# The mLSTM state stores of a hybrid diffusion trunk step: both directions of a head in one PSUM tile, one copy and one store each of C and n

## The chip, the cores and the metric

The kernel runs on one core of a Trainium2 chip. The metric is the device time of one execution, in microseconds (us). Profiles come from one profiled execution. In them PE is TensorE's matmul, PEld its weight load, DVE VectorE, ACT ScalarE, POOL GpSimd and SP SyncE, the engine whose queue issues nearly all DMAs of this kernel.

## The reference

One denoising step of one trunk layer, for two groups of tokens: 512 latent tokens of one request (which use a cache of context) and 128 context tokens of another (which start from empty states and leave new ones). The hidden size is 1024, all in fp32. A normalised and modulated input `h` goes through one wide projection `h @ w_in`, whose columns feed four mixers side by side and the gates:

- MLA, attention over a compressed key-value latent;
- mLSTM in both directions, 4 heads with keys of 64 and values of 128;
- windowed attention with grouped heads (SWA);
- RWKV-7 in both directions.

Their outputs are projected, gated and added, and a squared-ReLU MLP follows. The part around the change is the end of the mLSTM, for the context tokens. Per direction and head, with an empty state before, it is

```python
wk    = jnp.exp(g - m_new[..., None])
C_new = decay[..., None, None] * C + jnp.einsum('bhs,bhsd,bhsv->bhdv', wk, kc, vc)
n_new = decay[..., None] * n + jnp.einsum('bhs,bhsd->bhd', wk, kc)
```

so the new C is a product of weighted keys and values (64x128), and the new n the sum of the weighted keys (64). The outputs `new_mlstm_C` and `new_mlstm_n` have the shapes (1, 1, 2, 4, 64, 128) and (1, 1, 2, 4, 64): direction, head, key, value.

## The kernel before, in words

**Products.** Projections in fp32 are made as three products of halves: an operand is split into a high and a low part (`wh` and `wl` of a weight, `HH` and `HL` of `h`), and high by high, low by high and high by low are added in PSUM.

**Weights.** `load_split` (L583 to L594) loads a weight tile of 128x512 into `wr` (three buffers), ACT casts it to `wh` (L589), and DVE or POOL subtracts to get `wl` (L592).

**Stages.** The RWKV section comes first, then the mLSTM (L1208 to L1364), in whose time the windowed attention runs too (L1388 to L1510), then MLA (from L1512), then the gates and output projections, then the MLP. While the mixers run, TensorE has filling work: the gate columns of `h @ w_in`. These are tiles `pb` of 128x320 in PSUM, each 24 matmuls, two halves to a job (pb_4434 and pb_4435 are one job). A job's halves are copied out as `spb` by ACT (L833) and by DVE (L835), and stored to a scratch in DRAM by SP (L837, `gtd` and `mog`). There are two `pb` tiles of PSUM, so that a half can start only when the copy of the same half of the job before it is done.

**The mLSTM heads.** A loop over four heads (h), in a pool of SBUF `mh`. For each head the value tile `vt` (`mvt`) has two more columns of ones, so that one product of weighted keys `kw` (128x64) with `vt[:, 4, :]` (128x130) gives C in columns 0 to 127 and n in column 128. `pkt`, `pyb` and `pcf` share one PSUM tile, "my" of 128x512. At the end of a head, for each direction d: DVE weights the keys (`kw`, L1358), TensorE makes the product `pcf`, ACT copies it to `co` (L1362), and SP stores C (L1363, 64 rows of 512 bytes) and n (L1364, 64 elements of 4 bytes, one from each partition). `co` has one buffer, so the copy of the next direction waits until both stores of the last one have landed. `kw` and `jk` (a scratch that takes the squares of `hd`, whose sum is all that is used) have two buffers.

**After the heads.** When the pools `mp` and `mh` are closed, their SBUF goes to pools of the MLA section. Its first loads `ua` (L1553) go to such memory, so they wait until the last store of `co` has landed. From `ua` DVE copies the rotary columns `akr` (L1554), ACT makes sums of squares (`aj`, L1557 and L1558), DVE scales `ua` (L1561, L1562), and TensorE transposes it (`pal`).

**Order.** The instructions are not run in the order of the code. `order()` (L168 to L483) is a list scheduler: it takes all recorded instructions with their dependencies, gives each a duration from formulas (`cost()`, L127; DMAs by a start, an end and a rate, L38), and at each step places on a free engine the ready instruction with the longest path behind it. A DMA that stores from SBUF has 178.188 us added to that path, and a copy out of PSUM has 100. Every engine then executes its list strictly in that order, SP's list of DMA issues as well; a waiting instruction holds up all that stand behind it on its engine. The scheduler knows a DMA by its bytes alone, so it reckons with one and the same short time for the C stores and the n stores as for other small transfers.

Of the kernel before, what the change touches and what calls it, by code (L numbers as in the profile page):

```python
# [11 lines left out]
F32 = mybir.dt.float32  # L12
# [511 lines left out]
def build(nc, tc, I, O):  # L524
    V, A, G, PE, SY = nc.vector, nc.scalar, nc.gpsimd, nc.tensor, nc.sync
# [11 lines left out]
    def nm(s):  # L537
        uid[0] += 1
        return f"{s}_{uid[0]}"

    def mm(out, lhsT, rhs, start=True, stop=True):
        PE.matmul(out, lhsT, rhs, start=start, stop=stop)  # L542
# [308 lines left out]
    mps = mps_cm.__enter__()  # L851
# [360 lines left out]
    with pools(name="mp", bufs=1) as mp, pools(name="mps2", bufs=1, space=PSUM) as mps:  # L1212
# [54 lines left out]
        with pools(name="mh", bufs=1) as mh_:  # L1267
            for h in range(4):
                ht, rw = h // 2, slice((h % 2) * 64, (h % 2) * 64 + 64)
                if h % 2 == 0:  # L1270
                    qT = mh_.tile([128, T], F32, tag="mq", name=nm("mqT"))
                    kT = mh_.tile([128, T], F32, tag="mk", name=nm("mkT"))
                    SY.dma_start(qT, mqk[ht])
                    SY.dma_start(kT, mqk[2 + ht])
                    qsp = [mh_.tile([128, T], F32R, tag=f"mq{i}", name=nm("msp")) for i in range(2)]
                    ksp = [mh_.tile([128, 2, T], F32R, tag=f"mk{i}", name=nm("msp")) for i in range(2)]
                    split(*qsp, qT)
                    for i in range(2):
                        for x in ksp:
                            G.memset(x[hh[1 - i], i, :].bitcast(F32), 0.0)  # L1280
                        split(*(x[hh[i], i, :] for x in ksp), kT[hh[i]])
                vt = mh_.tile([128, NT, 130], F32, tag="mvt", bufs=2, name=nm("mvt"))
                G.memset(vt[:, :, 128:130], 1.0)
                SY.dma_start(vt[:, :, 0:128], mvd[:, ts_(h)].rearrange("(t p) n -> p t n", p=128))
                c0 = mh_.tile([128, 2, 130], F32, tag="mc0", bufs=2, name=nm("mc0"))
                G.memset(c0, 0.0)
                for d in range(2):
                    SY.dma_start(c0[rw, d, 0:128], I["state_mlstm_C"][0, 0, d, h])
                    SY.dma_start(c0[rw, d, 128:129], I["state_mlstm_n"][0, 0, d, h].unsqueeze(1))
                Mb, qs = [], []  # L1290
                for d in range(2):
                    M_ = mh_.tile([128, T], F32, tag="Mb", bufs=2, name=nm("Mb"))
                    SY.dma_start(M_, mdr[h, d].partition_broadcast(128))
                    e0 = mh_.tile([128, NS], F32, tag="e0", bufs=1, name=nm("e0"))
                    A.activation(e0, M_[:, 0:NS], AF.Exp, scale=-1.0, bias=m0b[:, d * 4 + h : d * 4 + h + 1])
                    q_ = mh_.tile([128, NS], F32, tag="qs", bufs=2, name=nm("qs"))
                    G.tensor_tensor(q_, e0, qT[:, 0:NS], op=ALU.mult)
                    Mb.append(M_)
                    qs.append(q_)
                Ps = []  # L1300
                for i in range(5):
                    nf = 512 - 128 * i if i < 4 else 128
                    nb = 128 * (i + 1) if i < 4 else 128
                    t0 = 0 if i < 4 else NS
                    ps = mps.tile([128, 512], F32, tag="ms", name=nm("pms"))
                    n = 512 if i < 4 else 128
                    mm3(ps[:, :n], [x[:, h % 2, ts_(i)] for x in ksp], [x[:, t0 : t0 + n] for x in qsp])
                    P_ = mh_.tile([128, 640], F32, tag="P", bufs=6, name=nm("P"))
                    o = 128 * i if i < 4 else 0
                    A.activation(P_[:, 0:nf], Mb[0][:, t0 + o : t0 + o + nf], AF.Exp, scale=-1.0, bias=tk[:, i * 16 + h : i * 16 + h + 1])  # L1310
                    A.activation(P_[:, nf : nf + nb], Mb[1][:, t0 : t0 + nb], AF.Exp, scale=-1.0, bias=tk[:, i * 16 + 4 + h : i * 16 + 5 + h])
                    G.affine_select(P_[:, 0:128], P_[:, 0:128], pattern=[[1, 128]], compare_op=ALU.is_ge, fill=0.0, base=0, channel_multiplier=-1)
                    G.affine_select(P_[:, nf + nb - 128 : nf + nb], P_[:, nf + nb - 128 : nf + nb], pattern=[[-1, 128]],
                                    compare_op=ALU.is_ge, fill=0.0, base=0, channel_multiplier=1)
                    V.tensor_tensor(P_[:, 0:nf], P_[:, 0:nf], ps[:, o : o + nf], op=ALU.mult)
                    V.tensor_tensor(P_[:, nf : nf + nb], P_[:, nf : nf + nb], ps[:, 0:nb], op=ALU.mult)
                    Ps.append((P_, nf))
                yo = mh_.tile([128, T], F32, tag="myo", bufs=1, name=nm("yo"))
                for j in range(5):
                    ps = mps.tile([128, 512], F32, tag="mo", name=nm("pmo"))  # L1320
                    for d in range(2):
                        out = ps[:, d * 130 : d * 130 + 130]
                        seq = []
                        if j < 4:
                            seq.append((qs[d][:, ts_(j)], c0[:, d, :]))
                            for i in (range(0, j + 1) if d == 0 else range(j, 4)):
                                P_, nf = Ps[i]
                                o = (j - i) * 128 if d == 0 else nf + j * 128
                                seq.append((P_[:, o : o + 128], vt[:, i, :]))
                        else:  # L1330
                            P_, nf = Ps[4]
                            seq.append((P_[:, d * 128 : d * 128 + 128], vt[:, 4, :]))
                        for n, (l, r) in enumerate(seq):
                            mm(out, l, r, start=(n == 0), stop=(n == len(seq) - 1))
                    dn = mh_.tile([128, 2], F32, tag="dn", bufs=4, name=nm("dn"))
                    A.activation(dn, ps[:, 128:260:130], AF.Abs)
                    V.tensor_tensor(dn, dn, tk[:, j * 16 + 8 + h : j * 16 + 16 : 4], op=ALU.max)
                    V.reciprocal(dn, dn)
                    hd = mh_.tile([128, 128], F32, tag="hd", bufs=2, name=nm("hd"))
                    A.activation(hd, ps[:, 0:128], AF.Copy, scale=dn[:, 0:1])  # L1340
                    V.scalar_tensor_tensor(hd, ps[:, 130:258], dn[:, 1:2], hd, op0=ALU.mult, op1=ALU.add)
                    jk = mh_.tile([128, 128], F32, tag="jk", bufs=2, name=nm("jk"))
                    s_ = mh_.tile([128, 1], F32, tag="s_", bufs=2, name=nm("s_"))
                    A.activation(jk, hd, AF.Square, accum_out=s_)
                    rsqrt(mh_, s_, s_, 128, eps6)
                    V.tensor_scalar(hd, hd, s_, None, op0=ALU.mult)
                    ps = mps.tile([128, 512], F32, tag="my", name=nm("pyb"))
                    transp(ps[:, 0:128], hd)
                    A.activation(yo[:, ts_(j)], ps[:, 0:128], AF.Copy, scale=pk("mln"))
                SY.dma_start(yT[1, h], yo)  # L1350
                ps = mps.tile([128, 512], F32, tag="my", name=nm("pkt"))
                if h % 2 == 0:
                    ktok = mh_.tile([128, 128], F32, tag="ktok", bufs=1, name=nm("ktok"))
                    transp(ps[:, 0:128], kT[:, NS:T])
                    A.copy(ktok, ps[:, 0:128])
                for d in range(2):
                    kw = mh_.tile([128, 64], F32, tag="kw", bufs=2, name=nm("kw"))
                    V.tensor_scalar(kw, ktok[:, rw], tk[:, 80 + d * 4 + h : 81 + d * 4 + h], None, op0=ALU.mult)  # L1358
                    ps = mps.tile([128, 512], F32, tag="my", name=nm("pcf"))
                    mm(ps[0:64, 0:130], kw, vt[:, 4, :])  # L1360
                    co = mh_.tile([64, 130], F32, tag="co", bufs=1, name=nm("co"))
                    A.copy(co, ps[0:64, 0:130])  # L1362
                    SY.dma_start(O["new_mlstm_C"][0, 0, d, h], co[:, 0:128])  # L1363
                    SY.dma_start(O["new_mlstm_n"][0, 0, d, h].unsqueeze(1), co[:, 128:129])  # L1364

    def swap_ap(ap, q, which):
        return ap.rearrange("p h (a b q) -> p h a b q", b=2, q=q)[:, :, :, which, :]
# [516 lines left out]
```

## Time and profile before

| | us |
|---|---|
| runs of the kernel before: median of 3 | 1817.38 |
| lowest, highest of them | 1809.24, 1836.86 |
| the profiled execution: its own time | 1829.33 |
| span in its profile, first to last instruction | 1827.4 |
| TensorE matmul busy in it | 1742.4 (95%) |
| ACT busy | 716.9 (39%) |
| DVE busy | 968.7 (53%) |

The mean granted TensorE clock was 0.96 of full speed. The profiled execution is 12 us longer than the median of the runs. The stores in question lie between 811 and 936 us of the span. The profile's columns: a group or tile row gives the line, engine, operation, output<-input and the count; a timeline row gives the start, the length in us, the engine, the line and in brackets the idle time of that engine ahead of it and what ended it; a chain row the start, the length and what ran; a window row its bounds, then its length, then for PE, PEld, DVE, ACT and POOL the busy time and (x) the number of instructions, then the granted TensorE clock, the busy share of the DMA engines and the GB/s.

### The profile page before, as it was taken

What the parts mean: (1) busy time and instruction counts of PE and PEld (TensorE: products, weight loads), DVE (VectorE), ACT (ScalarE), POOL (GpSimd) and SP (SyncE); (2) the same over time, 40 slices, a digit from 0 to 9 for tenths busy, and PEclk for the clock granted to TensorE, in tenths of its full rate; (3) what the DMA queues carried; (4) which work ended last, traced back from release to release, by engine and by line L of the source; (5) the groups of instructions that cost most, each with busy time, mean ns of one, the idle gap of its engine ahead of it and who ended that gap; (6) DMA issues with size and microseconds to landing.
All of it is one profiled execution on the core that took longest, in us unless ns stands there. A gap on an engine that the chain in (4) does not pass through costs nothing.

```text
span 1827.4 us, 32001 instructions
## 1 busy us (share of the span) xinstructions
PE 1742.4 (95%) x11923; PEld 1551.1 (85%) x11923; DVE 968.7 (53%) x2250; ACT 716.9 (39%) x1711; POOL 471.9 (26%) x488
## 2 busy tenths in 40 slices
PE   6999899999999987999989999899999999999998
PEld 3998788888888876878887999799889899898997
DVE  4236937586363348665548654367744334343342
ACT  5543242333223224675635643354434223132231
POOL 3455543354233223331222211005100010202012
PEclk9999999898679998999999999999999999999999
DMA  8554352344224354533363211576512222222222
GB/s 291 153 180 122 103 132 74 90 118 108 64 59 122 114 170 149 168 89 65 86 159 105 74 41 56 167 253 221 173 45 81 68 77 70 81 76 75 76 74 94
DMA packets 243211, 206.66 MB, mean 113 GB/s; under 512 B 46086, under 2 KB 194360, under 8 KB 243056
## 3 DMA queue, kind: packets, MB, share of 16 engines
q1 hardware_dynamic: 242416, 204.07, 38.2%
q8 instruction: 94, 1.54, 0.4%
q0 software_dynamic: 640, 0.56, 0.1%
q14 instruction: 61, 0.50, 0.1%
HBM read 163.08 MB, written 41.49 MB: 112 GB/s over the span
## 4 chain that ended last, share of the span: by engine, by line
PE 57%; DVE 5%; DMA 5%; ACT 1%; issue 1%; SPq 0%; POOL 0%; POOLq 0%; DVEq 0%; ACTq 0%
PE pb L542 29%; PE pa L542 12%; PE pwo L542 2%; DMA out_new_mlstm_n<-co 2%; PE pst L542 2%; PE pas L542 2%; PE pat L542 2%; PE pat L565 1%; PE pso L542 1%; PE pmo L542 1%; PE psc L542 1%; PE pada L542 1%; DMA wr<-in_w_in 1%; PE pms L542 1%; PE pspt L565 0%
## 5 line engine op out<-in xcount | busy, mean ns | idle before, releaser
L542 PE MATMUL pb<-HH,wh 128*128 128x320 f32 x1328 | 364.1, 325 | 21.8 <-ACT spb L833 10.8
L542 PE MATMUL pb<-HL,wh 128*128 128x320 f32 x1328 | 359.5, 323 | 0.8 <-DVE HL L753 0.8
L542 PE MATMUL pb<-HH,wl 128*128 128x320 f32 x1328 | 356.0, 321 | 0.0
L589 ACT CAST wh<-wr 128x512 fp32r<-128x512 f32 (+2 forms) x298 | 183.5, 618 | 379.9 <-PE pa L542 144.2
L592 POOL TENSOR_TENSOR wl<-wr,wh 128x512 fp32r<-128x512 f32 (+2 forms) x139 | 187.4, 1352 | 415.0 <-ACT wh L589 307.8
L542 PEld LDWEIGHTS pb<-HH,wh 128*128 128x128 f32 x1328 | 237.5, 192 | 33.6 <-ACT spb L833 12.9
L542 PEld LDWEIGHTS pb<-HL,wh 128*128 128x128 f32 x1328 | 236.8, 192 | 7.3 <-issue 4.0
L542 PEld LDWEIGHTS pb<-HH,wl 128*128 128x128 f32 x1328 | 236.4, 192 | 6.3 <-issue 3.5
L592 DVE TENSOR_TENSOR wl<-wr,wh 128x512 fp32r<-128x512 f32 x159 | 117.4, 744 | 200.1 <-ACT wh L589 116.5
L1846 POOL TENSOR_TENSOR x<-x,yt 128x512 f32<-128x512 f32 x40 | 53.6, 1341 | 480.7 <-DVE yt L1845 473.7
L542 PE MATMUL pt<-wh,HH 128*128 128x256 f32 (+2 forms) x360 | 101.7, 318 | 7.8 <-DVE mift L860 5.4
L542 PE MATMUL pa<-wh,fh 128*128 128x512 f32 x320 | 108.1, 393 | 0.0
L542 PE MATMUL pa<-wh,fl 128*128 128x512 f32 x320 | 106.7, 393 | 0.0
L542 PE MATMUL pa<-wl,fh 128*128 128x512 f32 x320 | 104.9, 393 | 0.0
L542 PE MATMUL pt<-wh,HL 128*128 128x256 f32 (+2 forms) x360 | 97.9, 312 | 0.0
L542 PE MATMUL pt<-wl,HH 128*128 128x256 f32 (+2 forms) x360 | 96.8, 310 | 0.0
L1109 POOL TENSOR_SCALAR S<-S,DL 128x128 f32<-128x128 f32 x80 | 56.8, 714 | 126.9 <-DVE S L1124 100.3
L542 PEld LDWEIGHTS pt<-wh,HH 128*128 128x128 f32 x360 | 68.1, 206 | 13.6 <-DVE mift L860 3.0
L835 DVE COPY spb<-pb 128x320 f32<-128x320 f32 x46 | 22.4, 487 | 105.9 <-PE pb L542 105.7
L542 PE MATMUL pst<-VU,Am 128*64 128x64 f32 (+1 forms) x640 | 74.2, 242 | 0.9 <-DVE VU L1118 0.5
L542 PE MATMUL pb<-yh,wh 128*128 128x320 f32 x256 | 64.8, 318 | 10.0 <-ACT yh L1752 6.5
L542 PEld LDWEIGHTS pa<-wh,fh 128*128 128x128 f32 x320 | 60.1, 188 | 13.4
(535 smaller groups left out, 3587.0 us busy)
## 6 DMA issues: line engine op xcount, KB each, us to landing
wr<-in_mlp_w SPq DMA_DIRECT2D x128, 256.0 KB
wr<-in_w_in SPq DMA_DIRECT2D x122, 256.0 KB
wa<-in_ada_w SPq DMA_DIRECT2D x64, 256.0 KB
gtd<-spb SPq DMA_DIRECT2D x32, 320.0 KB
sg<-gtd SPq DMA_DIRECT2D x32, 320.0 KB
ara<-in_ada_w SPq DMA_DIRECT2D x16, 512.0 KB
sgd<-sg SPq DMA_DIRECT2D x16, 320.0 KB
la<-sgd SPq DMA_DIRECT2D x16, 320.0 KB
```

Of the source, the lines that this page charges most:

```text
L542: PE.matmul(out, lhsT, rhs, start=start, stop=stop)
L565: PE.transpose(out, in_, ident[: in_.shape[0], : in_.shape[0]])
L589: A.copy(hi[:, :n], raw[:, :n])
L592: e.tensor_tensor(lo[:, :n], raw[:, :n], hi[:, :n].bitcast(F32), op=ALU.subtract)
L835: V.tensor_copy(t[:, hs(h)], p)
L1109: G.tensor_scalar(sn, so_, DL[:, c : c + 1], None, op0=ALU.mult)
L1846: G.tensor_tensor(x2[tt][:, cs], x2[tt][:, cs], t, op=ALU.add)
```

## The change

The products of the two directions go to one PSUM tile, side by side in columns 0 to 129 and 130 to 259. One ACT copy takes both to a tile `co` of 64x2x130, which has two buffers. One DMA stores both directions' C (64x2x128), and one both directions' n (64x2x1). `kw` and `jk` have one buffer instead of two. The numbers over the four heads:

| | before | after |
|---|---|---|
| `kw` on DVE, `pcf` products (128x64 by 128x130) | 8, 8 | 8, 8 |
| `co` copies on ACT | 8 of 64x130 | 4 of 64x260 |
| C stores | 8 of 64x128 | 4 of 64x2x128 |
| n stores | 8 of 64 elements | 4 of 128 elements |

```diff
-                    jk = mh_.tile([128, 128], F32, tag="jk", bufs=2, name=nm("jk"))
+                    jk = mh_.tile([128, 128], F32, tag="jk", bufs=1, name=nm("jk"))
...
+                ps = mps.tile([128, 512], F32, tag="my", name=nm("pcf"))
                 for d in range(2):
-                    kw = mh_.tile([128, 64], F32, tag="kw", bufs=2, name=nm("kw"))
+                    kw = mh_.tile([128, 64], F32, tag="kw", bufs=1, name=nm("kw"))
                     V.tensor_scalar(kw, ktok[:, rw], tk[:, 80 + d * 4 + h : 81 + d * 4 + h], None, op0=ALU.mult)
-                    ps = mps.tile([128, 512], F32, tag="my", name=nm("pcf"))
-                    mm(ps[0:64, 0:130], kw, vt[:, 4, :])
-                    co = mh_.tile([64, 130], F32, tag="co", bufs=1, name=nm("co"))
-                    A.copy(co, ps[0:64, 0:130])
-                    SY.dma_start(O["new_mlstm_C"][0, 0, d, h], co[:, 0:128])
-                    SY.dma_start(O["new_mlstm_n"][0, 0, d, h].unsqueeze(1), co[:, 128:129])
+                    mm(ps[0:64, d * 130 : d * 130 + 130], kw, vt[:, 4, :])
+                co = mh_.tile([64, 2, 130], F32, tag="co", bufs=2, name=nm("co"))
+                A.copy(co, ps[0:64, 0:260].rearrange("p (d n) -> p d n", n=130))
+                SY.dma_start(O["new_mlstm_C"][0, 0, :, h].rearrange("d k v -> k d v"), co[:, :, 0:128])
+                SY.dma_start(O["new_mlstm_n"][0, 0, :, h].rearrange("d k -> k d").unsqueeze(2), co[:, :, 128:129])
```

Since the scheduler starts from other instructions, the order of all engines differs from the first head's stores to the gate stage; before and behind that it is the same. Two places follow.

**The last head's stores and the load of `ua`.** On SP before (a number behind a name is that of the tile; a `gtd` or `mog` store carries the `spb` tile that it stores):

```order
L588 DMA wr_4600<-in_w_in 128x4x128
L1363 DMA out_new_mlstm_C<-co_9699 64x128
L1364 DMA out_new_mlstm_n<-co_9699 64x1
L837 DMA gtd<-spb_4301 128x640
L588 DMA wr_4636<-in_w_in 128x4x128
L1363 DMA out_new_mlstm_C<-co_9707 64x128
L1364 DMA out_new_mlstm_n<-co_9707 64x1
L588 DMA wr_4666<-in_w_in 128x4x128
L1553 DMA ua_10870<-mld 128x416
L1553 DMA ua_10899<-mld 128x416
```

On SP now:

```order
L588 DMA wr_4570<-in_w_in 128x4x128
L1350 DMA yT<-yo_9527 128x640
L1363 DMA out_new_mlstm_C<-co_9687 64x2x128
L1364 DMA out_new_mlstm_n<-co_9687 64x2x1
L588 DMA wr_4600<-in_w_in 128x4x128
L837 DMA gtd<-spb_4301 128x640
L588 DMA wr_4636<-in_w_in 128x4x128
L1553 DMA ua_10850<-mld 128x416
L1553 DMA ua_10879<-mld 128x416
```

One pair of stores stands there instead of two, the load of `wr_4600` has moved behind it, and that of `wr_4666` has moved behind the `ua` loads. On ACT before, at the same place (`spb_4367` is the copy of pb_4368, `spb_4433` that of pb_4434):

```order
L833 COPY spb_4301<-pb_4302 128x320
L1362 COPY co_9699<-pcf_9697 64x130
L589 CAST wh_4533<-wr_4534 128x512
L1362 COPY co_9707<-pcf_9705 64x130
L589 CAST wh_4569<-wr_4570 128x512
L833 COPY spb_4367<-pb_4368 128x320
L589 CAST wh_4599<-wr_4600 128x512
L1557 ACTIVATE aj_10873,asa_10874<-ua_10870 128x256
L1558 ACTIVATE aj_10873,asa_10874<-ua_10870 128x128
L833 COPY spb_4433<-pb_4434 128x320
```

On ACT now, from the copy of pb_4368 on; the one copy `co_9687` stands four rows ahead of it:

```order
L833 COPY spb_4367<-pb_4368 128x320
L1557 ACTIVATE aj_10853,asa_10854<-ua_10850 128x256
L1558 ACTIVATE aj_10853,asa_10854<-ua_10850 128x128
L1557 ACTIVATE aj_10882,asa_10883<-ua_10879 128x256
L1558 ACTIVATE aj_10882,asa_10883<-ua_10879 128x128
L1596 ACTIVATE kj_11855,krr_11854<-akr 128x32
L572 ACTIVATE rst_10859<-rsv_10858 128x2
L1596 ACTIVATE kj_11960,krr_11959<-akr 128x32
L573 ACTIVATE asa_10854<-rst_10859 128x2
L589 CAST wh_4599<-wr_4600 128x512
L572 ACTIVATE rst_10888<-rsv_10887 128x2
```

The cast of `wr_4600` moved from ahead of the first `ua` work to behind it, and the copy of pb_4434 from between the first `ua` tile's work and the second's to behind both (four rows behind the last one shown).

**The first uses of `ua` on DVE and PE.** On DVE before (`spb_4367` here is the copy of pb_4369, the second half of the job):

```order
L835 COPY spb_4301<-pb_4303 128x320
L835 COPY spb_4367<-pb_4369 128x320
L1554 COPY akr<-ua_10870 128x32
L1554 COPY akr<-ua_10899 128x32
L1559 TENSOR_SCALAR asa_10874<-asa_10874 128x1
```

On DVE now:

```order
L1359 TENSOR_SCALAR kw_9684<-ktok_9437,mtk 128x64
L835 COPY spb_4301<-pb_4303 128x320
L1554 COPY akr<-ua_10850 128x32
L1554 COPY akr<-ua_10879 128x32
L835 COPY spb_4367<-pb_4369 128x320
```

The two copies out of `ua` stand ahead of the copy of pb_4369 instead of behind it. On PE before, around the first transposes of `ua`:

```order
L542 MATMUL pb_4501<-HL,wh_4503 128x320
L542 MATMUL pb_4500<-HL,wh_4533 128x320
L565 MATMUL pal_10869<-k_68,ua_10870 128x128 x3
L542 MATMUL pb_4501<-HH,wl_4502 128x320
L542 MATMUL pb_4500<-HH,wl_4532 128x320
L542 MATMUL pb_4501<-HH,wh_4503 128x320
```

On PE now:

```order
L542 MATMUL pb_4435<-HH,wh_4437 128x320
L542 MATMUL pb_4434<-HH,wl_4466 128x320
L565 MATMUL pal_10849<-k_68,ua_10850 128x128 x3
L542 MATMUL pb_4435<-HL,wh_4437 128x320
L542 MATMUL pb_4434<-HH,wh_4467 128x320
L542 MATMUL pb_4435<-HH,wl_4436 128x320
```

They moved from the job of pb_4500 to the one before it, pb_4434; 20 rows ahead of them now stands the first row of pb_4435, which needs DVE's copy of pb_4369.

## The prediction

> **What bounds the kernel now.** I read the page first, then the rows of the tile `co`, the chain of waits around the stores, the TensorE timeline and the windows there. From the page, the busy time of TensorE and its weight loads and the chain by lines:
>
> ```profile
> PE 1742.4 (95%) x11923; PEld 1551.1 (85%) x11923; DVE 968.7 (53%) x2250; ACT 716.9 (39%) x1711; POOL 471.9 (26%) x488
> PE pb L542 29%; PE pa L542 12%; PE pwo L542 2%; DMA out_new_mlstm_n<-co 2%; PE pst L542 2%; PE pas L542 2%; PE pat L542 2%; PE pat L565 1%; PE pso L542 1%; PE pmo L542 1%; PE psc L542 1%; PE pada L542 1%; DMA wr<-in_w_in 1%; PE pms L542 1%; PE pspt L565 0%
> ```
>
> TensorE is the bound: 95% of a span of 1827.4 us. The only store with a share of the chain is the n store, 2%. So the change can gain what TensorE idles around it, and no more. The tile `co` and who sat idle for it:
>
> ```profile
> L1362 ACT COPY co<-pcf x8: 261/261/262, 811.4 to 927.3; 64x130 f32<-64x130 f32 x8
> L1363 SPq DMA_DIRECT2D out_new_mlstm_C<-co x8: 466/472/518, 811.6 to 927.6; - x8
> L1364 SPq DMA_DIRECT2D out_new_mlstm_n<-co x8: 588/588/1389, 812.2 to 928.2; - x8
>   DMA out_new_mlstm_n<-co: 13.5, 4
> ```
>
> With one buffer, the second direction's copy waits for the first direction's n store: four times, 13.5 us of ACT. The chain shows how long such a store takes (start, length); its last row here is from SP's timeline, an issue:
>
> ```profile
> 795.46 3.00 DMA wr<-in_w_in
> 812.19 7.26 DMA out_new_mlstm_n<-co
> 850.16 7.51 DMA out_new_mlstm_n<-co
> 892.74 6.88 DMA out_new_mlstm_n<-co
> 902.78 7.56 DMA wr<-in_w_in
> 920.22 7.02 DMA out_new_mlstm_n<-co
> 928.15 7.59 DMA out_new_mlstm_n<-co
> 937.24 3.43 DMA wr<-in_mla_w_uq
> 900.50 0.59 SPq L1364 DMA_DIRECT2D out_new_mlstm_n<-co  x1
> ```
>
> Five n stores of 256 bytes take 6.88 to 7.59 us, middle 7.26; a 256 KB weight load takes 3.00. The load issued at 902.78, 2.3 us behind the n store of 900.50, takes 7.56 and so lands at 910.34: what stands behind an n store lands after it. What reaches TensorE are its gaps (in brackets, length and releaser):
>
> ```profile
> 821.53 0.43 PE L542 MATMUL pso<-svS,sPT 128*128 128x64 f32 x2 [0.54 <-ACT sPT L1494]
> 858.63 0.69 PE L542 MATMUL psc<-skT,sqT 128*128 128x384 f32 x1 [2.77 <-ACT sP L1488]
> 900.01 0.33 PE L565 MATMUL pyb<-k,hd 128*128 128x128 f32 x1 [0.83 <-ACT co L1362]
> 911.39 0.33 PE L565 MATMUL pspt<-k,sP 128*128 128x128 f32 x1 [1.72 <-ACT sP L1488]
> 928.49 0.41 PE L542 MATMUL pb<-HH,wh 128*128 128x320 f32 x1 [1.15 <-ACT spb L833]
> 941.20 0.64 PE L542 MATMUL pb<-HH,wh 128*128 128x320 f32 x1 [5.45 <-ACT spb L833]
> ```
>
> Together 12.46 us. The first three and the fifth are ACT stopped at `co`; the fourth is ACT stopped at the late weight load (its wait row is below); the sixth is the MLA section, whose first load `ua` needs the closed pool's memory and so the last n store. In four-us windows (busy time of PE, PEld, DVE, ACT, POOL; then the granted clock):
>
> ```profile
> 856.00:860.00 4.00, 1.37 (x6) 1.29 (x6) 0.33 (x2) 1.81 (x7) 0.00 (x0) 0.82 0.51 53
> 860.00:864.00 4.00, 4.00 (x20) 3.92 (x19) 1.39 (x5) 1.75 (x7) 0.00 (x0) 0.50 0.00 0
> 864.00:868.00 4.00, 4.00 (x29) 3.99 (x29) 0.97 (x5) 1.07 (x5) 0.00 (x0) 0.83 0.55 89
> 932.00:936.00 4.00, 3.75 (x26) 3.49 (x24) 0.00 (x0) 0.00 (x0) 0.00 (x0) 1.00 0.53 28
> 940.00:944.00 4.00, 2.80 (x10) 2.80 (x11) 2.06 (x11) 3.81 (x20) 0.40 (x1) 0.56 0.35 94
> 944.00:948.00 4.00, 4.00 (x19) 3.99 (x19) 3.58 (x15) 0.41 (x1) 2.19 (x2) 0.59 0.61 198
> ACT wh L589 <- DMA wr<-in_w_in: 2.7, 1, 2.7
> ```
>
> After the two longest gaps the clock falls: (0.18+0.50+0.17)×4 = 3.4 us lost after 858, and (0.44+0.41)×4 = 3.4 after 941. All that this place can give is 12.5+6.8 = 19.3 us, 1.1%.
>
> **The change part by part.** *Two `co` buffers, one copy per head.* Four copies of 0.26 us go, the other four double in width: nothing on ACT, which is 39% busy. The 13.5 us of waits go, since the heads' copies are 27 us or more apart (the stores at 812, 850, 892 and 920), and the store before has long landed. With them go the gaps 0.54, 2.77, 0.83 and, after the second, 3.4 of clock: **7.5 us**. They don't come back at once: what is next for ACT there is score and spill work whose operands TensorE has already made.
>
> *Half the stores.* Eight SP issues fewer (four of 0.47, four of 0.59 us), on a queue that waits for nothing but data: nothing. What matters is how long a merged n store of 128 elements occupies the queue, and no row shows one. Bounds: one store of 64 elements, 7.26, and two, 14.5. I take the lower, being the row it resembles in form (same partitions, same queue, the two halves at separate places of the output), and keep the other as a rival.
>
> The Trainium skill speaks on both sides here. "DMA: Bandwidth & Descriptors", Rules for kernel authors, says that many small transfers should be merged into one; the same list says that a last dimension that isn't contiguous becomes one descriptor per element, and Specifications that transfers below 512 B are done as read-modify-write. By the second pair the 512 four-byte elements cost the same in four stores as in eight, and the merged store takes about 14.5 us, and the sum below would be 3.1 where I come to 11.2; the trace agrees with it so far as 256 bytes take 7.26 us and 256 KB take 3.00.
>
> At the lower bound, the third head's store is issued near 894 and has landed by 901, ahead of the load that was late at 910: its gap goes, **1.7 us**.
>
> *The order after the last store.* Here the written order changes for the worse. DVE's copies `akr` of the new `ua` tiles now stand ahead of the spill copy of pb_4369, which frees the PSUM tile of pb_4435; the first transposes `pal` stand inside pb_4434, where they stood behind the end of pb_4435; ACT's spill of pb_4434 stands behind the norms of both `ua` tiles. So TensorE meets the load at two new places. The rows that size it (SP, ACT, DVE and PE timelines, and two rows of tile views):
>
> ```profile
> L542 PE MATMUL pcf<-mvt,kw x16: 274/300/325, 810.9 to 920.3; 128*64 128x130 f32 x16
> L1358 DVE TENSOR_SCALAR kw<-ktok,mtk x8: 243/246/255, 809.9 to 893.5; 128x64 f32<-128x64 f32 x8
> 812.19 0.59 SPq L1364 DMA_DIRECT2D out_new_mlstm_n<-co  x1
> 935.86 0.82 SPq L1553 DMA_DIRECT2D ua<-mld  x2
> 939.90 0.42 ACT L1557 ACTIVATE aj<-ua 128x256 f32<-128x256 f32 x1 [9.27 <-DMA ua<-mld]
> 940.20 0.31 DVE L1554 COPY akr<-ua 128x32 f32<-128x32 f32 x2 [9.46 <-DMA gtd<-spb]
> 930.25 0.49 DVE L835 COPY spb<-pb 128x320 f32<-128x320 f32 x1 [8.04 <-PE pb L542]
> 947.58 0.49 PE L565 MATMUL pal<-k,ua 128*128 128x128 f32 x3
> ```
>
> In the clock of before, without what was gained earlier: the last `pcf` runs at 920.3; from the first `pcf` (810.9) to its n store (812.19) it is 1.3 us, so the merged store is issued at 921.6 and lands at 928.9; `ua` is issued then and is there 4.0 us later (935.86 to 939.90), at 933.0. TensorE has 75 rows from the last `pcf` to the first of pb_4435, at 3.75/26 = 0.145 us (window 932:936) 10.9 us: it arrives at 931.2. DVE's `akr` and spill take 0.31+0.49 from 933.1, so it goes on at 934.0: a gap of 2.8 us. Twenty rows on, at 936.9, stand the transposes, which need the normalised `ua`: before that took 947.58−939.90 = 7.7 us with DVE and ACT doing other work between; the parts on ACT and DVE alone are perhaps 4 (my estimate from some ten operations of 0.2 to 0.4 us such as the rows above). That is 937.0 to 940.7, a gap of 0.1 to 3.8; I take 1. So 3.8 us of gaps stand where 1.15+5.45 = 6.6 stood: **2.8 us** gained (0 to 3.7). The gap of 2.8 is as long as the one at 858, so I leave the clock's 3.4 us as lost.
>
> *One `kw` buffer.* The second direction's product now waits until the first `pcf` is done, and its `pcf` stands six rows (0.9 us) behind the first. In those fit the 0.30 of `pcf` and the 0.25 of `kw`, if DVE is free; if not, TensorE waits. Between 0 and 0.5 per head; I take 0.2, **−0.8 us**. *One `jk` buffer:* ACT writes it and nobody reads it: nothing.
>
> *Later.* All orders differ up to the gate stage, near 1250 us. Up to there TensorE is full, and at the gates it is not:
>
> ```profile
> 1040.00:1170.00 130.00, 130.00 (x1017) 128.99 (x1016) 66.60 (x174) 49.20 (x125) 12.92 (x11) 1.00 0.21 61
> 1180.00:1190.00 10.00, 2.89 (x14) 1.12 (x6) 4.35 (x7) 6.68 (x11) 0.00 (x0) 0.81 1.03 358
> 1188.86 1.44 PE L542 MATMUL pb<-yh,wh 128*128 128x320 f32 x4 [6.32 <-ACT yh L1752]
> ```
>
> The loads there (`so`, `yb`, `sg`) stand in another order; the DMA engines are full (1.03), so the bytes decide more than their order. I take 0, with a gap of 6.3 us gone or doubled as bounds.
>
> Sum: 7.5+1.7+2.8−0.8 = 11.2 us. The profiled execution took 1829.33 us (1827.4 span and 1.9 around it), so it becomes 1818; it lies 12 us above the median of the runs, 1817.4, and taken off that one, 11.2 gives **1806**.
>
> **The rivals.** *Per element (the merged store takes two stores' time, 14.5 us).* For it: a transfer of 256 bytes that takes longer than one of 256 KB pays by something other than bytes. Against it: that could be a latency which two halves share. Then ACT's waits still go (7.5), about half of the third head's 1.7 stays, and at the last head `ua` comes 7.3 us later, at 940.3: DVE holds TensorE from 931.2 to 941.3, 10.1 us, and the transposes 1 more, 11.1 against 6.6. Sum: 7.5+0.9−4.5−0.8 = 3.1, so 1814. It is the case that the Trainium skill's rule on one descriptor per element gives ("DMA: Bandwidth & Descriptors", Rules for kernel authors).
>
> *Slower: the merged store takes three stores' time, 22 us,* say because its halves' writes obstruct each other. Each us beyond 14.5 then lengthens the stop at `ua`; the 3.1 us are used up at 17.6 us, which is the point from which it decides. At 22 the last head loses 7.3 more, and the third head's store, issued near 894, holds its weight loads until about 917, where they came at 910.34: some 6 more. Sum −10: 1828. For it only that nothing like it was measured; against it that the five pieces of the chain differ by under 10%, as if nothing obstructed them.
>
> *The gaps go, the time doesn't.* TensorE is full from 1040 to 1170 with filling work; if the time won at 858 to 941 is spent in other waits, at the gate stage above all, where DMA is full, nothing is left: 1817. Against it: the loads of that stage follow from the mixers' end, which moves with TensorE. That the change doesn't do what it says is excluded for the copies and stores, whose numbers are fixed; the order is a matter of the list scheduler, and is as told.
>
> **How the numbers follow.** Forecast 0.46 (1806), per element 0.32 (1814), time not gained 0.13 (1817), slower 0.09 (1828). The range: low, everything at this place goes with its clock (19.3) and the gate's gap too (6.3): 1817.4−25.6 = 1792. High: no gain and the gate's gap once more, 1817.4+6.3 = 1824, which takes in the per-element case with its bounds; the slower rival lies outside. 2%, about what a measurement of this kernel can tell from no change, is 36 us, nearly twice all that the place holds; the runs of before differ by 28 us among themselves. So faster 0.03 and slower 0.03, for a median disturbed in one direction or an order gone far wrong, and 0.94 within.
>
> **What would show it.** Right: no wait of ACT's `co` for a DMA; no gap at the second head and a clock of 1.00 behind it; the merged n store 7 to 9 us long in the chain; a gap of 2 to 4 us at the first pb_4435, its releaser DVE's spill. Wrong: n stores of 13 us or more, TensorE stopped for about 10 us ahead of the MLA section, or new gaps between 1040 and 1210.

## The result, and the profile after

The changed kernel takes 1800.05 us (median of 20 runs, 1793.05 to 1821.52), the kernel before 1826.98 us (20 runs, 1807.81 to 1843.46). The ratio is 0.9893, with a 95% interval of 0.9863 to 0.9923: 19.5 us less, where the forecast was 11.2 less. The ratio is worked out from the fast runs of both kernels alone and is not that of the two medians, which lie 26.9 us apart.

The kernels' profiled executions differ by up to 28 us before anything that the change touches: the first transposition `pmt` of the mLSTM started between 699 and 727 us in all of them, at the same written work; the clock granted to TensorE up to there was 0.95 in the shortest (buf2_again, below) and 0.90 in the longest (the changed kernel's first profile). So they are compared by the stretch in which the order can differ, from the first `pmt` to the last product of the gate stage (`pb<-yh,wl`). The profile of the changed kernel shown here is one taken beside the first experiments, since the first one had 21 us more ahead of the stretch, at a lower clock. (TensorE's orders of before and after first differ 23 us behind the first `pmt`, some 70 us ahead of the first head's stores, and so earlier than the text on the change says.) The tile views give the ends of the stretch, and the last transposition `payt` of MLA inside it; each first and last start is in the middle of a row. Before:

```profile
L565 PE MATMUL pmt<-k,mR x10: 198/198/264, 715.8 to 731.3; 4*128 4x4 f32 x10
L565 PE MATMUL payt<-k,ayq x20: 270/272/278, 1066.0 to 1171.1; 128*128 128x128 f32 x20
L542 PE MATMUL pb<-yh,wl x256: 304/309/468, 1191.0 to 1314.2; 128*128 128x320 f32 x128
```

After:

```profile
L565 PE MATMUL pmt<-k,mR x10: 198/198/264, 705.8 to 720.9; 4*128 4x4 f32 x10
L565 PE MATMUL payt<-k,ayq x20: 270/272/281, 1036.1 to 1140.9; 128*128 128x128 f32 x20
L542 PE MATMUL pb<-yh,wl x256: 305/308/468, 1161.3 to 1285.4; 128*128 128x320 f32 x128
```

1314.2−715.8 = 598.4 us became 1285.4−705.8 = 579.6, which is 18.8 less (the table below has unrounded starts): up to `payt` 20.2 less (455.3 to 435.1), behind it 1.4 more. The tile `co` after, and what it sat idle for:

```profile
L1362 ACT COPY co<-pcf x4: 365/370/371, 806.2 to 902.0; 64x260 f32<-64x260 f32 x4
L1363 SPq DMA_DIRECT2D out_new_mlstm_C<-co x4: 607/631/686, 806.6 to 902.4; - x4
L1364 SPq DMA_DIRECT2D out_new_mlstm_n<-co x4: 602/618/648, 807.3 to 903.0; - x4
  PE pcf L542: 1.1, 2
```

The 13.5 us of waits for the n store are gone. Of six gaps of TensorE at this place one is left, and three small ones stand at the gate stage where one of 6.32 us stood:

```profile
917.41 0.64 PE L542 MATMUL pb<-HH,wh 128*128 128x320 f32 x1 [5.38 <-DVE spb L835]
1158.38 0.59 PE L542 MATMUL pada<-modr,k 99*2 99x512 f32 x1 [0.79 <-ACT modr L715]
1160.95 0.41 PE L542 MATMUL pb<-yl,wh 128*128 128x320 f32 x1 [0.50 <-DVE yl L1753]
1166.19 0.42 PE L542 MATMUL pb<-yh,wh 128*128 128x320 f32 x1 [2.03 <-ACT yh L1752]
```

The first is the first row of pb_4435, with DVE's spill as its releaser, as forecast. It is longer than forecast (2.8), and in the chain of waits it is the n store and then the load, behind which come the twenty rows up to the transposes:

```profile
903.02 9.36 DMA out_new_mlstm_n<-co
912.85 3.84 DMA ua<-mld
917.41 5.10 PE pb L542 x20
```

The windows around it show the slower clock behind it, as before:

```profile
912.00:916.00 4.00, 0.04 (x1) 0.00 (x0) 0.00 (x0) 0.00 (x0) 0.00 (x0) 0.85 0.85 279
916.00:920.00 4.00, 2.58 (x10) 2.59 (x11) 2.73 (x13) 3.14 (x17) 0.68 (x1) 0.50 0.65 182
920.00:924.00 4.00, 4.00 (x25) 3.99 (x25) 3.13 (x20) 0.93 (x3) 1.10 (x3) 0.80 0.31 92
```

### The profile page after: what moved, and what is told of

Same layout as the page of the kernel before. It is cut to its first block, busy times and chain, and to the rows that moved or that the text cites. A ratio compares the mean times of both kernels' runs of the same rounds, so it can differ in the third digit from the quotient of the medians.

```text
span 1819.8 us, 31999 instructions
## 1 busy us (share of the span) xinstructions
PE 1747.7 (96%) x11923; PEld 1555.1 (85%) x11923; DVE 971.2 (53%) x2250; ACT 718.1 (39%) x1707; POOL 467.9 (26%) x488
## 4 chain that ended last, share of the span: by engine, by line
PE 56%; DVE 2%; DMA 2%; ACT 1%; issue 0%; POOL 0%; POOLq 0%; SPq 0%; DVEq 0%; ACTq 0%
PE pb L542 27%; PE pa L542 12%; PE pwo L542 3%; PE pas L542 2%; PE pmo L542 2%; PE pat L542 2%; PE pada L542 1%; PE psc L542 1%; PE pso L542 1%; PE pat L565 1%; PE pspt L565 1%; PE pms L542 1%; PE pq L542 1%; PE pkv L542 0%; DMA out_new_mlstm_n<-co 0%
## 5 line engine op out<-in xcount | busy, mean ns | idle before, releaser
L542 PE MATMUL pb<-HH,wh 128*128 128x320 f32 x1328 | 362.7, 325 | 19.3 <-DVE spb L835 9.8
L542 PEld LDWEIGHTS pt<-wh,HL 128*128 128x128 f32 x360 | 69.5, 212 | 3.1
L542 PEld LDWEIGHTS pt<-wl,HH 128*128 128x128 f32 x360 | 69.3, 211 | 2.7 <-issue 0.4
```

## The experiments

Twelve runs followed. All but bench, which has only the stores in common with the kernel, are compared with the kernel before on the same chip. The theory to start from: the n store's long landing is what all the time went to; it held ACT through the one `co` buffer, and it holds MLA's first load. The rivals were the number of stores, the order in which DVE and SP do their work, or a cost per element. All the results but bench's are in one table (stretch: from the tile views as above; cover: rows of TensorE in the written order between the last `payt` and the first product of the gate stage; gate gap: TensorE's longest gap between the two):

| kernel | ratio to before (95%) | stretch, us | gap at MLA's start | cover, rows | gate gap |
|---|---|---|---|---|---|
| before | 1 | 598.5 | 1.15 and 5.45 | 60 | 6.32 |
| changed: again | 0.9906 (0.9870 to 0.9941) | 579.7 | 5.38 | 108 | 0.79 |
| b_row | 0.9868 (0.9834 to 0.9902) | 578.7 | 0.78 | 60 | 7.03 |
| a_row | 0.9885 (0.9847 to 0.9923) | 572.9 | 0.60 and 0.70 | 108 | 0.85 |
| gate_new | 1.0090 (1.0056 to 1.0125) | 605.3 | 2.08 and 6.01 | 60 | 10.06 |
| buf2 | 0.9838 (0.9793 to 0.9883) | 573.0 | 3.40 | 86 | 0.96 |
| buf2_again | 0.9850 (0.9796 to 0.9904) | 572.9 | 3.00 | 86 | 0.97 |
| akr_pool | 0.9913 (0.9878 to 0.9949) | 580.0 | 6.24 | 108 | 0.79 |
| nrow | 0.9865 (0.9821 to 0.9910) | 571.3 | 0.42 | 116 | 0.84 |
| merge_co1 | 0.9891 (0.9850 to 0.9932) | 578.1 | 4.67 | 108 | 0.92 |
| kwjk1 | 1.0013 (0.9976 to 1.0051) | 604.5 | 2.01 and 5.10 | 38 | 8.87 |
| brow | 0.9872 (0.9808 to 0.9936) | 582.4 | 0.38 and 0.78 | 53 | 8.41 |

Without the long waits at `co` the stretch repeats within 2 us (577.9 in the changed kernel's first profile, 579.7, and 578.1 in merge_co1, whose written order is the same; 573.0 and 572.9 for buf2); the whole time doesn't. With them it repeats less well: gate_new, whose orders are those of before up to the gate stage, took 460.1 us up to `payt` where before took 455.3, with n stores of 6.63 to 8.60 us in its chain. Where the ratio and the stretch disagree by a few us, as for a_row and b_row, the stretch is the finer measure, but differences to before are good to some 5 us only.

### The store alone

**again.** The changed kernel, without an edit.

> The changed kernel once more, on the same chip as the next three, so that they have it beside them. Both theories: about 0.989 of the kernel before (some 19 us less). In its profile one gap of TensorE of 4 to 5 us ahead of the MLA section, and merged n stores of 7 to 8 us.

The ratio, 0.9906, is as expected. The gap at MLA's start, 5.38 us, and the last n store, 9.36, were longer than that.

**b_row.** The kernel before, with another source for the n store:

```diff
-                    SY.dma_start(O["new_mlstm_n"][0, 0, d, h].unsqueeze(1), co[:, 128:129])
+                    SY.dma_start(O["new_mlstm_n"][0, 0, d, h].unsqueeze(0), co[0:1, 0:64])
```

> The kernel before, in its own order on every engine; only each n store's source is another: 64 neighbouring elements of one partition of co instead of one element from each of 64 partitions (the values stored as n are then not n but a row of C). Theory (the long landing of the n stores is what all the gaps between 811 and 941 come from): the store lands in about 2 us, ACT hardly waits at co, the six gaps (12.5 us) and the two clock drops (6.8) go, the gap at the gate stage stays: 0.989 to 0.991. Rival (a store of 256 bytes takes some 7 us whatever its layout, or the one buffer is the cause and not the time of the store): gaps as before, 1.000.

Measured 0.9868, more than expected, and 19.8 us off the stretch (0.8 of them ahead of the first store, where the granted clock was higher: 0.91 in the first 20 us, against 0.76). With one buffer and eight stores still there, the waits at `co` are gone (tile view), and the gate's gap stands as before (timeline):

```profile
L1362 ACT COPY co<-pcf x8: 252/262/263, 794.7 to 895.4; 64x130 f32<-64x130 f32 x8
  DMA out_new_mlstm_C<-co: 0.3, 1
1154.24 0.63 PE L542 MATMUL pb<-yh,wh 128*128 128x320 f32 x1 [7.03 <-ACT yh L1752]
```

So the cause is the time of the store; neither the buffer nor the number of stores costs by itself. The prediction's 19.3 us for all that the place holds agrees with this.

**a_row.** The same in the changed kernel (source `co[0:1, :, 0:64]`).

> The changed kernel, in its own order; its merged n store takes 2 x 64 neighbouring elements from one partition of co (again not the values of n). Theory (the last gap is the ua load held back by the last n store): store about 2 us, ua issued some 5 us earlier, the gap of 4 to 5 us and the slower clock behind it go: 5 to 8 us less than the changed kernel, 0.984 to 0.987. Rival (TensorE waits for the ua load's own time and for the order of DVE, not for the store): at most 1 us less, 0.989.

The stretch is 5 to 7 us shorter than the changed kernel's (572.9 against 577.9 to 579.7), in the expected range, and the gap of 5.38 us became two of 0.60 and 0.70 at the transposes, of which the first is:

```profile
910.93 0.30 PE L565 MATMUL pal<-k,ua 128*128 128x128 f32 x1 [0.60 <-issue]
```

The ratio, 0.9885, lies above the expected 0.984 to 0.987 and doesn't show it apart from the changed kernel's: the intervals overlap.

**bench.** What the landing hangs on, measured by itself.

```python
co = sb.tile([64, 1040], F32, tag="co", bufs=1)
A.copy(co, src)                      # waits until the store ahead has landed
SY.dma_start(dst, pick(co))          # one of the nine forms
```

> Only stores, each behind the copy that refills the one buffer it reads, so that the copy's wait shows the landing; nothing of the reference is computed, and only new_mlstm_C and new_mlstm_n are written, with ones. Each four times: 64 elements of 4 bytes from 64 partitions to neighbouring places (as n before), 128 to two such rows (as n after), 512 to eight rows, 2 x 64 from one partition, 64 elements to places 64 bytes apart and 512 bytes apart, 64 rows of 32 bytes, C of one direction and of two. Theory (elements that go to the same few lines of memory hold each other up, rows of their own don't): 64, 128 and 512 elements land in much the same 7 to 9 us, 512 bytes apart in 2 to 3, one partition in about 2, C in about 2. Rival (each element costs by itself, descriptors one after the other): 7 us for 64, about 13 for 128 and over 40 for 512, and 7 for the elements 64 or 512 bytes apart as well.

Waits of ACT in its profile, summed over four rounds, with the number and the longest (the name behind the arrow is the store that was waited for):

```profile
ACT row L538 <- DMA out_new_mlstm_n<-nAll: 36.6, 4, 10.3
ACT nAll L538 <- DMA out_new_mlstm_n<-nTwo: 29.2, 4, 8.0
ACT nTwo L538 <- DMA out_new_mlstm_n<-nOne: 28.9, 4, 7.7
ACT line L538 <- DMA out_new_mlstm_n<-row: 8.0, 4, 2.8
ACT cTwo L538 <- DMA out_new_mlstm_C<-cOne: 7.5, 4, 1.9
ACT page L538 <- DMA sc_line<-line: 7.1, 4, 1.8
ACT wide L538 <- DMA sc_page<-page: 7.0, 4, 1.7
ACT cOne L538 <- DMA sc_wide<-wide: 6.9, 4, 1.7
```

So 64 elements from 64 partitions (`nOne`) hold the buffer for 28.9/4 = 7.2 us, 128 (`nTwo`) for 7.3, 512 (`nAll`) for 9.2. The same 64 elements, when their places are 64 bytes (`line`) or 512 bytes apart (`page`), take 1.8 and 1.75; two rows of 64 from one partition (`row`) 2.0. The rival of a cost per element is refuted, by the 128 and by the 512, and so is one by size: 4-byte elements with places of their own are as quick as a C store (`cOne`, 1.9). (`line`, `page` and `wide` go to scratch in DRAM, the others to the outputs; that this isn't the cause is seen from `row` and `cOne`.) What is slow is 4-byte elements from different partitions to neighbouring places. Pieces of 32 bytes (`wide`) are not: 64 of them, from 64 partitions and to neighbouring places too, take 1.7. That the elements hold each other up at a shared line of memory fits all nine forms only if such a line has no more than 32 bytes; it was not shown directly.

The prediction weighed two rules of the Trainium skill's page "DMA: Bandwidth & Descriptors". Its Specifications say that transfers below 512 bytes are done as read-modify-write, and its Rules for kernel authors that a last dimension that isn't contiguous becomes one descriptor per element. Neither rule states a price; that the time goes with the number of elements was the prediction's reading, and the rows refute it: `page` has 64 elements of 4 bytes, a descriptor each by that rule, and lands in 1.75 us.

### Buffers and merging apart

**buf2.** The kernel before with `bufs=2` for `co`, and nothing else.

> The kernel before with one edit: two co buffers instead of one; still eight copies, eight C stores and eight n stores, in the order that the scheduler then writes. Theory (the gain at the stores comes from the copy's wait, which two buffers take away as well as merging): no wait of ACT's co for an n store, the first four gaps gone. Between the last transposes of MLA and the first product of the gate stage its order has 86 rows of filling work (60 before, 108 after), 3.8 us more cover, so the gate's gap falls to about 3 us: in all 10 to 16 us, 0.991 to 0.995. Rival (merging is what counts, eight slow stores occupy the queue as before): gaps from late loads stay, 0.996 to 1.000.

Measured 0.9838, a larger gain than expected, with 25.5 us off the stretch. The gate's gap is 0.96 us, where about 3 was forecast from the rows. ACT's copies wait for no store. Two n stores now stand in the queue at once, SP's timeline first and then the chain:

```profile
895.54 0.60 SPq L1364 DMA_DIRECT2D out_new_mlstm_n<-co  x1
896.97 0.59 SPq L1364 DMA_DIRECT2D out_new_mlstm_n<-co  x1
896.97 8.50 DMA out_new_mlstm_n<-co
906.41 2.80 DMA ua<-mld
911.13 0.63 PE L542 MATMUL pb<-HH,wh 128*128 128x320 f32 x1 [3.40 <-DVE spb L835]
```

The second, issued 1.4 us behind the first, lands 8.5 us after its issue; one behind the other would be 2×7.2−1.4 = 13. So they land beside each other, and eight stores cost no more here than four.

**buf2_again.** The same kernel once more.

> The kernel before with two co buffers, once more, for its interval beside that of the changed kernel. If two buffers do all that merging does: 0.985 to 0.991. If the last run's 0.984 was luck: 0.990 to 0.995.

0.9850, and 572.9 for the stretch: the first result was no luck.

**merge_co1.** The changed kernel with `bufs=1` for `co`.

> The changed kernel with one co buffer instead of two; the written order is the same on every engine. Theory (merged copies are 27 us and more apart, so a second buffer has nothing to do once they are merged): no wait of ACT's co for a store, the same gaps as the changed kernel, 0.988 to 0.992. Rival (the second buffer is needed): 4 to 8 us more than the changed kernel.

As expected (0.9891, stretch 578.1, no wait of the copy for a store). Of the two parts, merging and the second buffer, either alone removes the waits. By the stretch the second buffer alone takes 5 to 7 us less than both: its own gap at MLA's start is 3.0 to 3.4 us instead of 4.6 to 5.4; the rest lies in how the order came out, and was not taken apart.

**kwjk1.** The kernel before with `bufs=1` for `kw` and `jk`, which the change needed to make room.

> The kernel before with only kw and jk cut to one buffer, eight copies and stores and one co buffer as before. It tests two things. Gaps at the stores: as before, about 12 us, and with a kw that waits perhaps 1 more. The gate stage: its order leaves 38 rows of filling work between the last transposes of MLA and the first product of the gate stage (60 before, 108 in the changed kernel). Theory (the gap there is the time of the loads less the filling work that covers it): 22 rows of 0.145 us less cover, a gap of 9 to 10 us instead of 6.3, 1.000 to 1.004. Rival (SP's order decides, or the full DMA engines): gap 5 to 7 us.

No change that can be measured (1.0013). The gaps at the stores are there as before, some of them longer (15.7 us of waits of the copy `co` instead of 13.5, and a stretch 6.0 longer). The gate's gap is 8.87 us:

```profile
1191.16 0.63 PE L542 MATMUL pb<-yh,wh 128*128 128x320 f32 x1 [8.87 <-ACT yh L1752]
```

### The last gap ahead of MLA

**akr_pool.** The changed kernel with one line:

```diff
-                V.tensor_copy(kr[:, tt, :], u[:, 384:416])
+                G.tensor_copy(kr[:, tt, :], u[:, 384:416])
```

> The changed kernel with one edit: the copies akr out of ua run on POOL instead of DVE, so that DVE's spill of pb_4369 waits for nothing of ua; the orders of SP, ACT and PE are those of the changed kernel but for two rows. Theory (the load of ua, held back by the n store, is what TensorE waits for, wherever it meets it): the gap of about 5 us at pb_4435 goes and one of 4 to 6 us appears at the transposes pal, 20 rows on: 0 to 2 us less than the changed kernel, 0.988 to 0.990. Rival (DVE's order is the cause of that gap, as the prediction's step on the order after the last store has it): no gap over 1 us there, 5 to 8 us less, 0.985.

The gap left pb_4435 and came back at the transposes, 0.9 us longer:

```profile
929.65 0.45 PE L565 MATMUL pal<-k,ua 128*128 128x128 f32 x1 [6.24 <-DVE ua L1561]
```

The time is that of the changed kernel (0.9913, stretch 580.0). So DVE's order only sets where TensorE meets the late load, not how long it waits. Since a_row removes the gap, the cause is the n store ahead of `ua`.

**nrow.** The changed kernel with n made as a row on one partition (and `co` in one buffer, to make room):

```diff
                     mm(ps[0:64, d * 130 : d * 130 + 130], kw, vt[:, 4, :])
+                    mm(ps[0:1, 260 + d * 64 : 324 + d * 64], vt[:, 4, 128:129], kw)
...
-                SY.dma_start(O["new_mlstm_n"][0, 0, :, h].rearrange("d k -> k d").unsqueeze(2), co[:, :, 128:129])
+                nr = mh_.tile([1, 128], F32, tag="nr", bufs=1, name=nm("nr"))
+                A.copy(nr, ps[0:1, 260:388])
+                SY.dma_start(O["new_mlstm_n"][0, 0, :, h].unsqueeze(0), nr.rearrange("p (d k) -> p d k", d=2))
```

> The changed kernel with n made as a row: a second product per direction, ones (a column of vt) by kw, gives n as 64 neighbouring values on one partition, which ACT copies and one store of 2 x 64 elements from one partition writes; co has one buffer to make room. Theory (what is left of the cost is the landing of the n store from 64 partitions): the store lands in about 2 us, ua is there before TensorE needs it, no gap over 1 us ahead of MLA, eight more small products of 0.2 us or so and four copies: 4 to 8 us less than the changed kernel, 0.984 to 0.987. Rival (the extra work and the new order take it back): 0.989 or more.

The shortest stretch of all, 571.3, which is 7 to 8 us less than the changed kernel's; ratio 0.9865. No gap over half a us is left ahead of MLA:

```profile
911.96 0.33 PE L565 MATMUL pal<-k,ua 128*128 128x128 f32 x1 [0.42 <-DVE ckl L1547]
```

nrow and buf2 are both ahead of the changed kernel by the stretch, and by their ratios, though the intervals of both overlap with the changed kernel's. The two cannot be told apart.

**brow.** The kernel before, one buffer, eight stores, n as a row per direction.

> The kernel before, one co buffer and eight stores of each kind, but n made as a row (a second product per direction, ones by kw, a copy on one partition and a store of 64 neighbouring elements from it). Theory: n stores land in under 2 us, all gaps from the stores to MLA go (19 us) less some 2 for the added products; its order leaves 53 rows of filling work ahead of the gate stage, so the gap there stays at about 7: 0.989 to 0.992. Rival (the buffer or the number of stores is what costs): 0.996 or more.

The ratio is 0.9872, a larger gain than expected, the stretch 582.4, and the gaps from the stores to MLA are gone: none is over 0.8 us. The gate's gap is longer than expected:

```profile
1179.49 0.64 PE L542 MATMUL pb<-yh,wh 128*128 128x320 f32 x1 [8.41 <-ACT yh L1755]
```

### The gate stage

**gate_new.** The kernel before; after the scheduler has written the order, SP's list alone is rearranged.

```diff
+    so = [a for a in sp if to(a).startswith("so_") and ti(a).startswith("mog")][:2]
+    yb = [a for a in sp if to(a).startswith("yb_")][:4]
+    j0 = next(i for i, a in enumerate(sp) if to(a).startswith("sg_"))
+    sg = [a for a in sp if to(a).startswith("sg_")][:3]
+    for a in sg + so + yb:
+        sp.remove(a)
+    sp[j0:j0] = sg + so + yb
```

> The kernel before, with only SP's order at the gate stage changed: three sg, two so and the four yb loads stand ahead of the two weight loads of the mLSTM's output projection, as in the changed kernel; all other engines' orders, and the stores, are those of before. Theory (the gate stage's gap of 6.3 us comes from yb standing behind a weight load that waits for its buffer): the gap falls to 2 or 3 us and the clock behind it recovers, 4 to 8 us less: 0.996 to 0.998. Rival (the DMA engines are full there, so bytes decide): gap as before, 1.000.

The theory fell. The gap grew to 10.06 us, and the kernel got slower (1.0090). The chain shows the weight load, now behind nine loads, and the gap's end:

```profile
1182.21 7.32 DMA wr<-in_mlstm_w_o
1194.21 0.63 PE L553 MATMUL pb<-yh,wh 128*128 128x320 f32 x1 [10.06 <-ACT yh L1763]
```

ACT's cast of that weight stands ahead of the sigmoid of `so` in its order, so moving `yb` ahead only made something else the last. Why the whole kernel got slower is only in part known: its stretch is 6.8 us longer than before's, but 4.8 of them stand up to `payt`, ahead of the edit, and 2.0 behind it.

That left the question what shortens the gap in the changed kernel. In the chain the loads `yb` and `so` are as long after as before. Before:

```profile
1181.34 5.76 DMA yb<-yT
1188.08 4.41 DMA so<-mog
```

After:

```profile
1146.42 5.13 DMA sg<-gtd
1151.57 6.26 DMA yb<-yT
1158.80 4.58 DMA so<-mog
```

Counted from the last `payt`, `yb` starts no earlier than before (1181.34−1171.1 = 10.2 us, and 1151.57−1140.9 = 10.7). What changed is how long TensorE's filling work goes on: it ends near 1158 now, so 12 of the 16 us of these three loads lie under it. The written order has 108 rows between the last transposition `payt` and the first product of the gate stage, where the order of before has 60: 48 rows of 0.145 us are 7.0 us more cover. (The traces show the same 48: 98 matmuls of `pb` there instead of 50.) Over the kernels of the table the gap goes with the rows: 8.87 at 38, 8.41 at 53, 6.32 and 7.03 at 60, under 1 at 86 and more (with gate_new, whose loads were rearranged, as the exception). The price of a row is only rough: from the rows 9 to 10 was forecast for kwjk1, and 8.87 came; for brow about 7, and 8.41; for buf2 about 3, and 0.96. No run changed the cover alone, so it is well supported, not proved.

## Why the prediction was right, and where it was not

| step | forecast, us | measured, us |
|---|---|---|
| waits at `co`: gaps 0.54, 2.77, 0.83 and the clock's 3.4 | 7.5 | all gone: 7.5 |
| third head: late weight load | 1.7 | gone: 1.7 |
| last head and MLA's start: 6.6 to 3.8 | 2.8 | 6.6 to 5.38: 1.2 |
| one `kw` buffer | −0.8 | no gap of TensorE: 0 |
| elsewhere up to the last `payt` | none | 2.8 |
| gate stage | 0 | 5.6 |
| sum | 11.2 | 18.8 |

The split of the measured sum: up to the last `payt` the stretch is 20.2 us shorter, of which 7.0 is filling work that moved behind it: 13.2 for the stores and mixers. Behind it the stretch is 1.4 longer with that 7.0 in it: 5.6 gained. (This part is the firmer one: behind `payt` b_row, in the order of before, took 142.8 us, and before 143.2.) From the 13.2 the first four rows take 10.4; 2.8 are left. Of these 0.9 stand ahead of the first row at which the two orders differ, where the granted clock was 0.76 before and 0.89 after in the first 20 us, so they are no gain of the change; for the rest no cause is shown, and it is less than the 4.8 by which gate_new and before differ at the same order. In the other two profiles of the same written order the gap at MLA's start was 4.62 and 4.67, so 2.0 gained there instead of 1.2.

- **The bound and the size of the place** were right. b_row, with the order untouched, gained 19.8 us where 19.3 were estimated from the gaps and the clock, both drops of the clock included. That the two agree within 0.5 is luck in part, since the stretch of before is good to some 5 us only.
- **The length of the merged store** was the main uncertainty, taken at one store's 7.26 and not at 14.5. The last one took 8.0 and 9.4 us in two profiles of the changed kernel (9.0 in merge_co1), and in bench it is 7.3 against 7.2. The per-element rival (0.32) and the slower one, 22 us, are refuted.
- **The order after the last store.** That the gap would stand at pb_4435 with DVE's spill as its end was right, and that the clock's 3.4 stay lost. The gap was 1.8 to 2.6 us longer than the 2.8 at that place, and so were the store and the load ahead of it: from the store's issue to the arrival of `ua` 12.9 and 13.7 us passed (chain of the first profile, and 903.02 to 912.85+3.84 above), where 7.26+4.0 = 11.3 was reckoned. The second gap, 1 at the transposes, didn't come: behind the first gap the clock was at half (0.50 in the window from 916), so TensorE's twenty rows took 5.10 us (chain) instead of 2.9, in which time the work on `ua` could be done. The step's reading that the order of DVE makes it worse was wrong, as akr_pool showed.
- **Later: "I take 0, with a gap of 6.3 us gone or doubled as bounds".** This is the step that failed; it carries most of the difference between 11.2 and 19.5. The reason given, that DMA is full there and the bytes decide, leaves out that those loads run while TensorE still has filling work. The written order, known ahead, had the 48 rows; at 0.145 us each they are 7.0 us, enough to cover the gap of 6.3; 5.6 were gained. The step looked at the order of the loads, SP's list, where TensorE's list holds the rows. (That the cover is the cause is well supported, not proved, as said above.)
- **"The gaps go, the time doesn't"** (0.13) is refuted by the ratio's interval, 0.9863 to 0.9923.

The sign, the main mechanism and the range held; the size was short by 8 us, of which 5.6 is the gate stage's.

## What to carry to other kernels

When a change makes a list scheduler write a new order, count in the written order how much covering work stands between the last instruction that starts a stage's loads and the first that needs them, before and after, and price it at the rows' length from the trace; that moved more here than any step around the edit but the first, as far as the table above bears it out. Where a small store is slow and a buffer waits for it, try the second buffer alone before merging: here it did at least as much. Small states spread over partitions are better brought to one partition first, if a spare product or transpose can do it: in bench the store then took 2 us instead of 7.

## What the runs showed of the hardware

- Stores of 4-byte elements from 64 partitions to neighbouring places take 7.2 us for 64, 7.3 for 128 and 9.2 for 512 elements, against 1.75 to 1.8 when the places are 64 or 512 bytes apart, 2.0 from one partition, and 1.7 for neighbouring pieces of 32 bytes from 64 partitions (bench). The prediction had weighed a cost per element and a fixed one.
- Of two such stores issued 1.4 us apart (buf2), the second landed 8.5 us after its issue; one after the other it would have been some 13.
- The kernel's own time varied more by what lies ahead of the change than by the change: 699 to 727 us for the same work up to the mLSTM, at a granted clock of 0.95 to 0.90, while the stretch that held the change repeated within 2 us without the waits at `co`, and within some 5 with them.
